# A hybrid backbone block: the RWKV inverse takes its first masked product from LQ by four predicated copies of 32 rows on DVE

## The chip, the cores and the metric

The kernel runs on one core of one Trainium2 chip. The core has five engines that run side by side and wait for each other by semaphores: PE (TensorE: matrix products and transposes), DVE (VectorE), ACT (ScalarE), POOL (GpSimd) and SP (SyncE, which here only issues transfers). Each works through its own list of instructions in order. The metric is the device time of one execution in microseconds (us), the median of several.

## The reference

Two layers over 256 context tokens and 1024 latent tokens of width 1024. Each layer has a modulated RMSNorm, one input projection that feeds three groups, an output projection, and a SwiGLU feed-forward part:

```python
px_a, px_b, px_c = _split(px, (GLA_COLS, SWA_COLS, RWKV_COLS))
oa_c, oa_x = gla_group(...)     # chunked gated linear attention
ob_c, ob_x = swa_group(...)     # windowed softmax attention
oc_c, oc_x = rwkv_group(...)    # RWKV-7, both directions
xx = xx + g1x * (jnp.concatenate([oa_x, ob_x, oc_x], axis=-1) @ w_out[l])
```

The change lies in the RWKV group. Its recurrence, for each of four heads of width 64 and each of two directions, is

```python
sa = jnp.einsum('bhvk,bhk->bhv', S, kkt)
S = S * wt[:, :, None, :] - sa[..., None] * (kkt * at)[:, :, None, :] + vt[..., None] * kt[:, :, None, :]
o = jnp.einsum('bhvk,bhk->bhv', S, rt)
```

## The kernel before

All data is fp32; the big projections are split into a high and a low part (fp32r) and take three products each (`ps_in` for the input projection).

**The RWKV stage** (`rwkv_mixer`, one per layer) works on chunks of 64 tokens, 20 chunks per direction, and takes both directions and all heads together: a tile `[128, 4, 128]` holds four units `u` (two directions by two pairs of heads), with the two heads of a pair in the upper and lower 64 partitions. Inside a chunk the recurrence is a triangular system, and its inverse `X` is built by doubling: blocks of 1, 2, 4, ... rows are joined by masked products.

`prep()` runs once per chunk `i` and works on two chunks at a time, the young one (`i`) and the old one (`i - 1`). For the young one it makes, in this order: the products `AK` by `AK` on PE (`gram`, into `ps_g`), masked by DVE into `LQ`; the first joining step, which needs no product, since for blocks of one row the entries are those of `LQ` itself (the lines that change); and the transpose of `X` in blocks of 32, `XT`. For the old one it makes `MP` (another `gram`). Then come two joining steps for both chunks together, each of four parts that wait for each other: `ps_y` on PE (from `LQ` and `XT`), its copy `y` on ACT, `ps_w` on PE (from `y` and `X`), a predicated copy into `X` on DVE under the mask `lev2`, and again `XT`. Last, for the old chunk alone, the step from 32 to 64 rows (a short `ps_y` and `ps_w`, `KT`, `XF`).

The tiles `X` and `XT` are halves of `X2` and `XT2` `[128, 2, 4, 32]`: partition 32a + s holds row s of diagonal block a, with columns of 32. In `LQ` those diagonal blocks lie at columns `r % 64` of the rows from `r`, a different column offset for rows 0 to 31 and 64 to 95 than for 32 to 63 and 96 to 127. So the four groups of 32 rows have to be taken apart.

`scan()` runs one chunk behind: `ps_r` from `MP` and the values `Vbd` and from `AK` and the state `SBD`; its copy `Rbd` (half on DVE, half on ACT); `ps_r` again from `Rbd` and `XF`; the copies `VU` (DVE) and `Ubd` (ACT); `ps_s` from `VU` and `KT`; and DVE's sum into `SBD`, the state for the next chunk.

**What runs beside it.** The input projection of the other two groups (`in_rest`: `ps_in`, 24 products for each of its column blocks and groups of tokens) fills PE between the steps. Its results are drained by ACT, and some need more work: rotary positions (`t`, `in`, with a product on POOL at L657) and, ten times per layer, a unit of the GLA decay (`in_gla`, L690 to L730: `ps_gl` on PE, `gl_z` on DVE, four functions on ACT with two loads of function tables, `gl_z` and a running sum `gl_u` on DVE).

**What sets the order.** The order on PE in this stage is written by `Weave`: every job is a generator that yields the time it wants to wait, measured by a count `TE.t` of the nominal times of the products placed so far, and the next job taken is the one that is due first. So the number in a `yield` is a guess of how long the other engines need until the next product of this job can start, and PE's list is filled with other jobs' products for as long. `yield 3400` stands between the two `gram` calls and the first `ps_y`. The order on DVE, ACT, POOL and SP is chosen by a scheduler when the program is built; the operations of `prep` and `scan` are given priority (`FIRST`; their calls all show as L177 in the profile).

Of the kernel before, what the change touches and what calls it, by code (L numbers as in the profile page):

```python
# [10 lines left out]
F32 = mybir.dt.float32  # L11
# [27 lines left out]
P = 128  # L39
# [106 lines left out]
def block_kernel(ctx: ExitStack, tc: tile.TileContext, a):  # L146
    nc = tc.nc
    V, S, G, SY = nc.vector, nc.scalar, nc.gpsimd, nc.sync
# [973 lines left out]
    def rwkv_mixer(l, t_first, pool, fpool, pp, spawn):  # L1122
# [7 lines left out]
        lev1 = pool.tile([P, 128], U8, name="lev1")  # L1130
# [19 lines left out]
        f2 = lambda ap: ap.rearrange("p u n -> p (u n)")  # L1150
# [5 lines left out]
        def gram(AK, w_, dst):  # L1156
            V = FIRST[0]
            ps = new([P, 4, P], "ps_g")
            for u in range(4):
                for hs in H:  # L1160
                    TE.matmul(ps[hs, u, :], AK[hs, u, w_, :], AK[hs, u, 0:2, :].rearrange("p s n -> p (s n)"))
            V.tensor_tensor(dst.rearrange("p (d q) n -> p d q n", d=2), ps.rearrange("p (d q) n -> p d q n", d=2),
                            mgr.unsqueeze(2).to_broadcast([P, 2, 2, P]), ALU.mult)
# [3 lines left out]
        def load(i):  # L1167
            b, cc = batch[i], (i, SIGC[i])

            AK = pool.tile([P, 4, 4, 64], F32, name="AK", bufs=4)  # L1170
            for d in range(2):
                SY.dma_start(AK[:, 2 * d:2 * d + 2], d_ab[:, 2 * d:2 * d + 2, cc[d]])
            Dt = pool.tile([P, 4], F32, name="Dt", bufs=4)
            for d in range(2):
                G.tensor_copy(Dt[:, 2 * d:2 * d + 2].unsqueeze(2), Dall[l][:, 2 * d:2 * d + 2, cc[d]:cc[d] + 1])
            b.update(cc=cc, AK=AK, Dt=Dt)
# [6 lines left out]
        def prep():  # L1183

            V, S, G = FIRST
            load(0)
            for i in range(NC + 1):
                yield after(("s", i - 3))
                p = i % 2
                young, old = batch[i] if i < NC else None, batch[i - 1] if i else None  # L1190
                hv = slice(0, 2) if i < NC and i else slice(p, p + 1) if old is None else slice(1 - p, 2 - p)
                if young is not None:
                    if i + 1 < NC:
                        load(i + 1)
                    X, XT = X2[:, p], XT2[:, p]
                    G.tensor_copy(X, eye32.unsqueeze(1).to_broadcast([P, 4, 32]))
                    young["LQ"] = LQ = pool.tile([P, 4, P], F32, name="LQ", bufs=3)
                    gram(young["AK"], 3, LQ)
                    ld = pool.tile([P, 4, 32], F32, name="ld")
                    for r in range(0, 128, 32):  # L1200
                        S.copy(ld[r:r + 32], LQ[r:r + 32, :, r % 64:r % 64 + 32])
                    V.copy_predicated(f2(X), lev1, f2(ld))
                    V.transpose(f2(XT), f2(X))
                if old is not None:
                    cc, Dt, AK = (old[n] for n in ("cc", "Dt", "AK"))
# [12 lines left out]
                                    Dt.unsqueeze(2).to_broadcast([P, 4, P]), ALU.mult)  # L1218
                    old["MP"] = MP = pool.tile([P, 4, P], F32, name="MP", bufs=2)
                    gram(AK, 2, MP)  # L1220
                yield 3400 if young is not None else 0
                both = [(h, b["LQ"]) for h, b in ((p, young), (1 - p, old)) if b is not None]
                for step in range(2):
                    py = new([P, 2, 4, 32], "ps_y")
# [17 lines left out]
                X, XT, LQ, xf = X2[:, 1 - p], XT2[:, 1 - p], old["LQ"], XF[p]  # L1242
# [113 lines left out]
        for rank, gen in ((0, scan()), (1, prep()), (3, finish_all())):  # L1356
            spawn(gen, rank, LEAD[l])
# [582 lines left out]
```

## Time and profile before

| | |
|---|---|
| median of 3 runs | 3725.89 us (3722.07 to 3726.19) |
| profiled execution | 3736.55 us, of which the span of the profile is 3734.3 us |
| PE busy | 3554.6 us, 95% of the span |
| DVE busy | 2378.2 us, 64% |
| ACT busy | 1498.3 us, 40% |
| POOL busy | 706.5 us, 19% |

Busy times are sums over an engine's instructions. Several small products of PE overlap in its array, so many matmuls can share one stretch of busy time. An engine's idle time costs something only where PE, or the work that ends last, waits for it.

### The profile page before, as it was taken

The numbers are of one execution on the slowest core, as the hardware profiler recorded it, in microseconds if no ns is written. First come the engines' busy times: TensorE is split into PE (matmuls) and PEld (weight loads), VectorE is DVE, ScalarE is ACT, GpSimd is POOL, SyncE is SP. The second block draws the span as 40 slices with busy tenths as digits, with TensorE's granted clock in tenths as the row PEclk, the third lists the DMA queues.
The fourth block names the chain that finished last, engine by engine and source line by source line (L and its number), as shares of the span: only waits on it lengthen the run. The fifth ranks groups of instructions, "written<-read, shape, count | busy, mean of one in ns | idle before, by whom it ended". The sixth has DMA issues, their size and how long they took to land. (4 is left out here: it accounts for less than half of the span.)

```text
span 3734.3 us, 76148 instructions
## 1 busy us (share of the span) xinstructions
PE 3554.6 (95%) x30714; PEld 2821.1 (76%) x30714; DVE 2378.2 (64%) x4596; ACT 1498.3 (40%) x3014; POOL 706.5 (19%) x979
## 2 busy tenths in 40 slices
PE   7998999999999999999999998889899999999998
PEld 4767778656688888888888766778777778888787
DVE  4764556556557777746776783455665576666766
ACT  4434543346324333333442553543366153333213
POOL 3122332111323000000332232232211340000002
PEclk9999999999999999999999999999989999999999
DMA  5253443552331333325421234343321332221511
GB/s 183 105 170 101 116 133 95 144 147 84 98 108 58 110 113 112 114 71 197 130 91 58 87 136 151 111 149 93 94 74 53 102 108 94 82 88 57 203 63 62
DMA packets 310767, 405.77 MB, mean 109 GB/s; under 512 B 52880, under 2 KB 210192, under 8 KB 308368
## 3 DMA queue, kind: packets, MB, share of 16 engines
q1 hardware_dynamic: 310416, 400.92, 34.2%
q8 instruction: 242, 3.96, 0.5%
q14 instruction: 109, 0.89, 0.1%
HBM read 290.54 MB, written 105.03 MB: 106 GB/s over the span
## 5 line engine op out<-in xcount | busy, mean ns | idle before, releaser
L160 PE MATMUL ps_in<-h,w_hl 128*128 128x512 f32 (+1 forms) x2928 | 712.1, 384 | 10.4 <-ACT w_hl L412 3.3
L160 PEld LDWEIGHTS ps_in<-h,w_hl 128*128 128x128 f32 x2928 | 490.0, 194 | 128.5 <-issue 43.3
L160 PE MATMUL ps_gu<-f,hl 128*128 128x512 f32 (+1 forms) x2400 | 567.3, 389 | 7.4 <-DVE hl L413 4.1
L160 PE MATMUL ps_d<-g,w_hl 128*128 128x512 f32 (+1 forms) x2688 | 557.5, 369 | 8.4 <-DVE x L1704 5.9
L160 PEld LDWEIGHTS ps_d<-g,w_hl 128*128 128x128 f32 x2688 | 464.2, 189 | 102.2 <-DVE x L1704 10.5
L160 PEld LDWEIGHTS ps_gu<-f,hl 128*128 128x128 f32 x2400 | 442.9, 190 | 101.2 <-DVE hl L413 5.0
L1704 DVE SCALAR_TENSOR_TENSOR x<-ps_d,mods,x 128x512 f32<-128x512 f32 (+1 forms) x448 | 290.7, 683 | 132.3 <-PE ps_d L160 131.8
L160 PE MATMUL ps_gu<-T,hl 128*128 128x512 f32 x1440 | 346.8, 390 | 1.4 <-DVE u L1605 1.4
L160 PEld LDWEIGHTS ps_gu<-T,hl 128*128 128x128 f32 x1440 | 268.7, 188 | 57.6 <-ACT g L412 1.8
L277 POOL TENSOR_TENSOR ada<-ada 128x256 f32<-128x256 f32 x112 | 90.6, 841 | 690.0 <-DMA x<-d_gt 558.3
L365 POOL TENSOR_TENSOR nacc<-nacc,nsq 128x512 f32<-128x512 f32 (+1 forms) x52 | 60.8, 1170 | 758.5 <-ACT nsq L364 743.5
L412 ACT CAST hl<-S 128x512 fp32r<-128x512 f32 x160 | 98.4, 620 | 250.3 <-PE ps_gu L160 156.4
L412 ACT CAST w_hl<-w_raw 128x1024 fp32r<-128x1024 f32 (+1 forms) x100 | 100.9, 1013 | 237.4 <-PE ps_d L160 200.1
L412 ACT CAST hl<-raw 128x512 fp32r<-128x512 f32 x156 | 96.7, 623 | 221.4 <-PE ps_gu L160 194.6
L1044 DVE TENSOR_REDUCE mx<-ps_ss 128x1 f32<-128x640 f32 (+2 forms) x144 | 107.4, 747 | 118.0 <-PE ps_ss L160 117.5
L160 PE MATMUL ps_o<-m,w_hl 128*128 128x512 f32 (+1 forms) x720 | 173.1, 388 | 0.0
L413 DVE TENSOR_TENSOR hl<-S,hl 128x512 fp32r<-128x512 f32 x160 | 109.9, 689 | 65.2 <-ACT hl L412 64.8
L160 PEld LDWEIGHTS ps_o<-m,w_hl 128*128 128x128 f32 x720 | 126.8, 194 | 32.5 <-issue 8.2
L413 DVE TENSOR_TENSOR w_hl<-w_raw,w_hl 128x1024 fp32r<-128x1024 f32 (+1 forms) x100 | 120.1, 1204 | 37.0 <-ACT w_hl L412 36.8
L413 DVE TENSOR_TENSOR pT<-ps_st,pT 128x512 fp32r<-128x512 f32 (+1 forms) x168 | 108.9, 656 | 32.9 <-ACT pT L412 32.4
L160 PEld LDWEIGHTS ps_x<-f,hl 128*128 128x128 f32 x960 | 124.5, 191 | 6.6 <-issue 0.8
L160 PE MATMUL ps_x<-f,hl 128*128 128x256 f32 x960 | 127.1, 283 | 0.0
(354 smaller groups left out, 5993.3 us busy)
## 6 DMA issues: line engine op xcount, KB each, us to landing
w_raw<-in_w_in_dram SPq DMA_DIRECT2D x44, 512.0 KB, 3.8
raw<-in_w_gate_dram SPq DMA_DIRECT2D x44, 512.0 KB, 4.1
raw<-in_w_up_dram SPq DMA_DIRECT2D x44, 512.0 KB, 3.6
x<-d_gt SPq DMA_DIRECT2D x88, 256.0 KB, 3.7
AK<-d_ab SPq DMA_DIRECT2D x80, 256.0 KB, 3.6
w_raw<-in_w_down_dram SPq DMA_DIRECT2D x40, 512.0 KB, 4.2
d_gt<-u SPq DMA_DIRECT2D x68, 256.0 KB, 2.0
d_ab<-W SPq DMA_DIRECT2D x16, 1024.0 KB, 4.1
```

The costliest lines, as they stand in the source:

```text
L160: return nc.tensor.matmul(out, lhsT, rhs, **kw)
L277: G.tensor_tensor(acc[:, s], acc[:, s], ps_[n % 2], ALU.add)
L365: (G if 0 < o < 5 else V).tensor_tensor(self.acc[g0], self.acc[g0], sq[:, :n], ALU.add)
L412: S.copy(dst[:, 0], src)
L413: V.tensor_tensor(dst[:, 1], src, dst[:, 0].bitcast(F32), ALU.subtract)
L1044: V.tensor_reduce(m_, psf[:, :nk * P], AX.X, ALU.max)
L1704: V.scalar_tensor_tensor(x[:, o, g0:g0 + n], ps[:, :n], mods[:, l, s, 40 + o:41 + o], x[:, o, g0:g0 + n], ALU.mult, ALU.add)
```

## The change

The copy of the four diagonal blocks into `ld` on ACT is dropped. Instead of one predicated copy of 128 rows from `ld`, DVE makes four of 32 rows straight from `LQ`, each with its own column offset. The pause that `prep` asks for between the `gram` products and the first `ps_y` goes from 3400 to 2600.

```diff
                     young["LQ"] = LQ = pool.tile([P, 4, P], F32, name="LQ", bufs=3)
                     gram(young["AK"], 3, LQ)
-                    ld = pool.tile([P, 4, 32], F32, name="ld")
                     for r in range(0, 128, 32):
-                        S.copy(ld[r:r + 32], LQ[r:r + 32, :, r % 64:r % 64 + 32])
-                    V.copy_predicated(f2(X), lev1, f2(ld))
+                        V.copy_predicated(X[r:r + 32], lev1[r:r + 32].rearrange("p (u n) -> p u n", n=32),
+                                          LQ[r:r + 32, :, r % 64:r % 64 + 32])
                     V.transpose(f2(XT), f2(X))
...
-                yield 3400 if young is not None else 0
+                yield 2600 if young is not None else 0
```

The new pause moves products on PE in both RWKV stages, and the scheduler's order on the other engines moves with them. Elsewhere the two programs stand in the same order but for a few rows at the beginning of the softmax attention that follows.

On PE, in the iteration for chunk 14 of the first layer, this stood between the products for LQ and MP (`ps_g`) and the scan's last product (`ps_in` is fill; 128x512 is a wide one):

```order
L160 MATMUL ps_g<-AK 64x128 x16
L160 MATMUL ps_in<-h_288,w_hl 128x256 x7
L160 MATMUL ps_r<-Vbd_1818,MP 128x128 x4
L160 MATMUL ps_r<-SBD,AK 128x128 x4
L160 MATMUL ps_in<-h_334,w_hl 128x512 x5
L160 MATMUL ps_y<-XT_1828,LQ 32x32 x32
L160 MATMUL ps_r<-Rbd,XF_1820 128x128 x4
L160 MATMUL ps_in<-h_334,w_hl 128x512
L160 MATMUL ps_w<-X_1827,y 32x32 x32
L160 MATMUL ps_in<-h_334,w_hl 128x512 x4
L160 MATMUL ps_s<-VU,KT 128x128 x4
L160 MATMUL ps_r<-Ubd,LQ 128x128 x4
```

And in the same place of the changed program:

```order
L160 MATMUL ps_in<-h_334,w_hl 128x512 x3
L160 MATMUL ps_r<-Vbd_1818,MP 128x128 x4
L160 MATMUL ps_r<-SBD,AK 128x128 x4
L160 MATMUL ps_in<-h_334,w_hl 128x512 x2
L160 MATMUL ps_y<-XT_1828,LQ 32x32 x32
L160 MATMUL ps_in<-h_334,w_hl 128x512 x3
L160 MATMUL ps_r<-Rbd,XF_1820 128x128 x4
L160 MATMUL ps_w<-X_1827,y 32x32 x32
L160 MATMUL ps_in<-h_334,w_hl 128x512 x2
L160 MATMUL ps_s<-VU,KT 128x128 x4
L160 MATMUL ps_r<-Ubd,LQ 128x128 x4
```

Three wide fill products that stood ahead of the first `ps_y` now stand behind it, ahead of `ps_r<-Rbd`; two of those that stood between `ps_w` and `ps_s` have gone to later places.

On DVE, in the iteration for chunk 3 of the first layer, from LQ to the copy of the second joining step, before (the rows of L703 to L722 belong to a GLA unit, `lev_1792` is the mask `lev1`):

```order
L177 TENSOR_TENSOR LQ<-ps_g,c_mgr 128x512
L177 TENSOR_TENSOR MP<-ps_g,c_mgr 128x512
L177 COPY_PREDICATED X_1827<-lev_1792,ld 128x128
L177 STREAM_TRANSPOSE XT_1828<-X_1827 128x128
L177 COPY Rbd<-ps_r 64x4x64
L703 TENSOR_SCALAR gl_z<-ps_gl,par 128x256
L707 SCALAR_TENSOR_TENSOR gl_z<-gl_z,gl_u 128x256
L712 SCALAR_TENSOR_TENSOR gl_u<-cst,gl_z 128x256
L177 COPY VU<-ps_r 64x512
L718 COPY dD<-gl_e 128x4
L722 TENSOR_TENSOR gl_e<-gl_e,gi 128x256
L177 COPY_PREDICATED X_1827<-lev_1793,ps_w 128x256
```

And in the changed program:

```order
L177 TENSOR_TENSOR LQ<-ps_g,c_mgr 128x512
L177 COPY_PREDICATED X_1827<-lev_1792,LQ 32x128 x4
L177 TENSOR_TENSOR MP<-ps_g,c_mgr 128x512
L177 STREAM_TRANSPOSE XT_1828<-X_1827 128x128
L177 COPY Rbd<-ps_r 64x4x64
L177 COPY VU<-ps_r 64x512
L177 COPY_PREDICATED X_1827<-lev_1793,ps_w 128x256
L177 STREAM_TRANSPOSE XT_1828<-X_1827 128x256
L703 TENSOR_SCALAR gl_z<-ps_gl,par 128x256
L177 TENSOR_TENSOR SBD<-ps_s,tmp 64x4x64 x2
L707 SCALAR_TENSOR_TENSOR gl_z<-gl_z,gl_u 128x256
L712 SCALAR_TENSOR_TENSOR gl_u<-cst,gl_z 128x256
```

MP has moved behind the four copies, and the GLA unit has moved from between `Rbd` and `VU` to either side of `SBD`. Over both layers, other groups' rows stand between `Rbd` and `VU` in 19 of 40 iterations before and in 9 after; L707 stands between the two in six of its twenty places before and in none after, when twelve are behind `SBD` and six between XT and `SBD`.

On PE, the last iteration of the second layer, in which only the old chunk is worked on, before:

```order
L160 MATMUL ps_g<-AK 64x128 x8
L160 MATMUL ps_r<-Vbd_22386,MP 128x128 x4
L160 MATMUL ps_r<-SBD,AK 128x128 x4
L160 MATMUL ps_y<-XT_22396,LQ 32x32 x16
L160 MATMUL ps_r<-Rbd,XF_22388 128x128 x4
L160 MATMUL ps_w<-X_22395,y 32x32 x16
L164 MATMUL ps_f<-cst,fy 128x128 x2
L160 MATMUL ps_s<-VU,KT 128x128 x4
L160 MATMUL ps_r<-Ubd,LQ 128x128 x4
L160 MATMUL ps_y<-XT_22396,LQ 32x32 x16
L160 MATMUL ps_w<-X_22395,y 32x32 x16
```

And in the changed program:

```order
L160 MATMUL ps_r<-SBD,AK 128x128 x4
L160 MATMUL ps_in<-h_20762,w_hl 128x512 x5
L160 MATMUL ps_y<-XT_22356,LQ 32x32 x16
L160 MATMUL ps_r<-Rbd,XF_22348 128x128 x4
L164 MATMUL ps_f<-cst,fy 128x128 x2
L160 MATMUL ps_w<-X_22355,y 32x32 x16
L160 MATMUL ps_in<-h_20762,w_hl 128x512 x4
L160 MATMUL ps_s<-VU,KT 128x128 x4
L160 MATMUL ps_r<-Ubd,LQ 128x128 x4
L160 MATMUL ps_in<-h_20762,w_hl 128x512
L160 MATMUL ps_y<-XT_22356,LQ 32x32 x16
L160 MATMUL ps_in<-h_20762,w_hl 128x512 x5
```

Fifteen wide fill products now stand in this iteration, where there were none; the number of fill products in the whole stage is the same.

## Rows read from the trace of the kernel before

**Rows 1.** Windows, first RWKV stage: us, busy time (instructions) by engine, PE's clock, DMA.

```profile
core 0 of [0], span 3734.3 us
...
255.00:682.00 427.00, 390.32 (x8034) 321.55 (x8035) 234.05 (x637) 181.63 (x438) 118.82 (x196) 0.96 0.38 111
```

**Rows 2.** Waits of PE, first stage: in total, times, longest (us).

```profile
PE ps_y L160 <- DVE XT L177: 11.7, 8, 3.3
PE ps_w L160 <- ACT y L177: 7.3, 7, 1.9
PE ps_s L160 <- DVE VU L177: 6.5, 5, 2.2
...
PE ps_r L160 <- ACT Ubd L177: 3.0, 3, 1.0
```

**Rows 3.** Waits of PE, second stage.

```profile
PE ps_y L160 <- DVE XT L177: 19.4, 9, 3.3
PE ps_r L160 <- ACT Rbd L177: 7.9, 6, 2.1
...
PE ps_w L160 <- ACT y L177: 5.4, 7, 1.3
```

**Rows 4.** Timeline of one iteration: start, us, engine, line, operation, [idle before].

```profile
609.02 0.69 DVE L177 TENSOR_TENSOR LQ<-ps_g,c_mgr 128x512 f32<-128x512 f32 x1 [0.58 <-PE ps_g L160]
...
609.80 1.22 ACT L177 COPY ld<-LQ 32x128 f32<-32x128 f32 x4 [1.33 <-DVE LQ L177]
609.89 0.69 DVE L177 TENSOR_TENSOR MP<-ps_g,c_mgr 128x512 f32<-128x512 f32 x1 [0.18 <-PE ps_g L160]
...
611.12 0.30 DVE L177 COPY_PREDICATED X<-lev,ld 128x128 f32<-128x128 uint8 x1 [0.54 <-ACT ld L177]
...
611.46 0.31 DVE L177 STREAM_TRANSPOSE XT<-X 128x128 f32<-128x128 f32 x1
...
613.60 0.75 PE L160 MATMUL ps_y<-XT,LQ 32*32 32x32 f32 x64
```

**Rows 5.** Tile XF: shortest/median/longest ns, first and last start.

```profile
L177 DVE TENSOR_TENSOR XF<-X,c_eye x80: 235/344/732, 289.0 to 2672.5; 32x128 f32<-32x128 f32 x80
```

**Rows 6.** Timeline, first and last of 13 iterations with little spare time.

```profile
386.82 0.31 DVE L177 STREAM_TRANSPOSE XT<-X 128x128 f32<-128x128 f32 x1
...
388.22 0.75 PE L160 MATMUL ps_y<-XT,LQ 32*32 32x32 f32 x64
...
2630.01 0.31 DVE L177 STREAM_TRANSPOSE XT<-X 128x128 f32<-128x128 f32 x1
...
2631.37 0.75 PE L160 MATMUL ps_y<-XT,LQ 32*32 32x32 f32 x64
```

**Rows 7.** Timeline, a GLA unit ahead of VU.

```profile
370.40 0.43 DVE L707 SCALAR_TENSOR_TENSOR gl_z<-gl_z,gl_u 128x256 f32<-128x256 f32 x1 [2.97 <-ACT gl_u L706]
...
371.59 0.68 DVE L177 COPY VU<-ps_r 64x512 f32<-64x512 f32 x1
...
372.32 1.16 PE L160 MATMUL ps_s<-VU,KT 128*128 128x128 f32 x8 [1.16 <-DVE VU L177]
```

**Rows 8.** Timeline, a load of function tables ahead of the copy y.

```profile
396.72 1.28 ACT L713 ACT_TABLE_LOAD   x1
...
398.88 0.90 PE L160 MATMUL ps_w<-X,y 32*32 32x32 f32 x64 [1.87 <-ACT y L177]
```

**Rows 9.** Timeline of PE at the end of the second stage.

```profile
2660.03 0.33 PE L160 MATMUL ps_y<-XT,LQ 32*32 32x32 f32 x16 [2.30 <-DVE XT L177]
...
2670.76 0.45 PE L160 MATMUL ps_w<-X,y 32*32 32x32 f32 x32 [0.40 <-ACT y L177]
...
2681.82 11.62 PE L160 MATMUL ps_in<-h,w_hl 128*128 128x512 f32 x48
```

**Rows 10.** Timeline, a predicated copy beside the rope product on POOL.

```profile
535.92 1.70 POOL L657 TENSOR_TENSOR in<-in,rope 128x512 f32<-128x512 f32 x1 [2.76 <-DMA t<-in]
...
536.41 1.38 DVE L177 COPY_PREDICATED X<-lev,ld 128x128 f32<-128x128 uint8 x1
```

## The prediction

> **What bounds the kernel now.** I read the page first: TensorE (PE) is busy in almost the whole span, so what counts is the time in which PE stands still. The edited lines run only in the two RWKV stages, one per layer, each about 427 us long; the windows view of the first shows PE busy in 390 us of them, ScalarE (ACT) in 182 us, VectorE (DVE) in 234 us [rows 1]. No engine but PE is near its limit there. What PE does in the stage is fixed: the same products stand in both programs. So the change can only move PE's waits, and the waits view says what they are: in the first layer 11.7 us for the transposed inverse XT, 7.3 us for ACT's copy `y`, 6.5 us for DVE's copy `VU` and 3.0 us for ACT's `Ubd` [rows 2]; in the second 19.4 us for XT, 7.9 us for `Rbd`, 5.4 us for `y` [rows 3]. All of it is some 61 us in 3734, and no single kind is long. The masked copies themselves are seen in one iteration of the timeline [rows 4]: LQ ends at 609.71, four ACT copies make `ld` (1.22 us) while DVE masks MP beside them, the predicated copy takes 0.30 us, the transpose 0.31 us and ends at 611.77, and the product that needs it starts at 613.60. There is 1.83 us to spare, and PE does not wait.
>
> **What the change does to the first step.** ACT loses four copies per iteration, 160 in all, 1.22 us per group. DVE loses one predicated copy of 0.30 us and gains four. The trace has none of 32 rows. The nearest row on the low side is DVE's 32-row subtraction of the same 128 elements at 0.235 us (its shortest), on the high side its median, 0.344 us [rows 5]; between them I take 0.30 us, the present copy's, since the free size is the same and only the rows are fewer. The four then take 1.2 us (0.94 to 1.38). DVE's new order puts MP behind them and ahead of the transpose in most iterations, so its 0.69 us, which lay beside `ld`, now lies in the chain: from LQ's end 0.05 + 1.20 + 0.69 + 0.04 + 0.31, about 2.3 us to the end of XT instead of 2.0 to 2.06 (2.03 to 2.47 by the bounds). The shorter pause also moves the first `ps_y` ahead of three wide fill products. 48 of those take 11.62 us [rows 9], so that is 0.72 us. The spare time shrinks by 1.0 us in each of 40 iterations. I read the spare, from the end of XT to the start of `ps_y`, in all 40: in 27 it is 1.14 us or more, mostly near 1.85, and there nothing happens. In 13 it is less, the first at 387.13 to 388.22, the last at 2630.32 to 2631.37 [rows 6]; the smallest, 0.14 us, is the hand-over itself. Adding up what is missing there (1.02 + 0.14 less the spare) gives 7.3 us of new waits, 4.5 us with the low price of the copy, 9.4 us with the high. In some of the 13 XT was late because `ld` stood behind other ACT work, which can't happen any more: **+6 us**. Queued behind the four copies on DVE are MP, XT and then `Rbd`; `Rbd` isn't wanted until the SBD products end, at about the moment when DVE now comes free, so I add nothing for it.
>
> **What moves with it.** The new pause shifts where the GLA units (`in_gla`, ten per layer, one DVE chain each that has to wait for ACT in its middle) fall into an iteration. Today five of them stand between `Rbd` and `VU` on DVE. The one at 370 us shows the price: DVE holds `gl_z` until ACT has made `gl_u`, `VU` starts only at 371.59, and `ps_s` on PE waits 1.16 us [rows 7]; VU and Ubd together are 9.5 us in the first layer. In the second, some 5 of the 7.9 us for `Rbd` lie ahead of the tail and come the same way. After the change no unit stands between the two. They stand around `SBD` instead, twelve behind it (eleven of them just ahead of the next masked copy), six ahead of it. There they cost too: in the iteration of 398.88 ACT is in a table load of 1.28 us when `ps_y` ends, and `ps_w` waits 1.87 us for `y` [rows 8]. Three of today's five units of that kind in the first layer pay this. So today's price is 9.5 + 5 + 3 x 1.9 + some 2 in the second layer, 22 us; if three in five of the eighteen pay 1.9 us it is 20.5 us: **-2 us**. The ends are far apart: -15 if the waits for VU, Ubd and Rbd go and nothing comes in their place, +12 if all eighteen pay.
>
> **The tail of the second layer.** The fill products run out there: the last iteration has none, and PE waits 2.30, 1.39 and 0.40 us, three times in all from 2660.03 to 2670.76 [rows 9]. The new order still has fill in that iteration, ahead of `ps_y`, `ps_s` and the last `ps_w`. I take the three as covered, **-4 us** (0 to -4.1).
>
> **ACT's relief.** 80 copies per layer at 1.22 us for four are 24 of 182 us, 13% of its work there. Of the 12.7 us that PE waits for `y` I take the same share, **-2 us** (0 to -6; the first `ps_w` also has three more products ahead of it).
>
> **Sum.** +6 - 2 - 4 - 2 = -2 us. The profiled execution took 3736.55 us around a span of 3734.3, so it would take 3734.5; the median of the runs shown is 3725.89, 10.7 us below it, and becomes **3724 us**. 0.2%, about what a measurement of this kernel can tell from no change, is 7.5 us.
>
> **A rule against the row.** In one iteration the predicated copy took 1.38 us instead of 0.30, in exactly the time in which GpSimd ran its rope product [rows 10]; a second of the 40 looks the same. The Trainium skill says why (SBUF — State Buffer, "Who interferes with whom"): VectorE with two SBUF inputs and GpSimd reading SBUF share a read interface, and whoever starts first keeps the other out. By that rule the four copies, which all have two SBUF inputs, offer the lock 1.2 us instead of 0.3 us per iteration. The row agrees; what it would cost here is a rival below.
>
> **The rivals.** *Slower, the GLA units (0.22).* Standing around SBD, each unit's table loads and its wait in DVE's queue meet `y` or the second masked copy, and each of the eighteen costs PE the 1.87 us of the one at 398.88. For it: eleven now stand in exactly that place. Against it: two of the five there today pay nothing. It is +12 + 6 - 4 - 2 = +12, 3738 us; it decides from about 1.6 us per unit on, where the sum passes +7.5. *Faster, the queues come clean (0.28).* With nothing between `Rbd` and `VU` in 31 of 40 iterations (21 now), the waits for VU, Ubd and Rbd go and none replaces them: -15 + 6 - 4 - 2 = -15, 3711 us. For it: they are the best understood waits in the trace. Against it: the units must run somewhere. *The lock (0.07).* If in each of the twenty iterations with a rope product a copy is held 1.08 us longer, that passes the remaining spare of 0.85 us by 0.23 us: 20 x 0.23 = 4.6 us more, 3728 or 3729 us. Against it: only two of 40 copies met one, and GpSimd is idle where they now stand in the iteration shown.
>
> **How the numbers follow.** The forecast, all terms small and of both signs, gets 0.43, with its own range 3716 to 3732. The range takes in most of both rivals, 3708 to 3741. Faster by over 0.2% is the clean-queue case and the forecast's low edge, 0.32; slower the GLA case, 0.22; within 0.2% the rest, 0.46.
>
> **What the new profile would show.** No `ld`; 160 predicated copies near 0.30 us, four in about 1.2 us; XT ending 2.3 us after LQ; waits of `ps_y` for XT at the first step in about a dozen iterations, of 0.2 to 1 us; the VU and Ubd waits of the first layer mostly gone, longer waits of `ps_w` for `y` and of the last `ps_y` for XT; no 2.30 us wait in the tail. ACT's busy time should fall by some 47 us and DVE's rise by about 36 us, neither of which is worth anything by itself. I am wrong if the 32-row copies take far from 0.30 us, if the waits around the GLA units don't keep their total, or if a stage changes in which nothing was edited.

## The result, and the profile after

The changed kernel takes 3746.33 us (3743.11 to 3750.85, four runs) against 3723.98 us for the kernel before on the same chip: a ratio of 1.0057 [1.0044, 1.0070]. It is 22.4 us slower by the medians and some 21 us by the ratio, outside the predicted range, on the side of the rival that was given 0.22.

The page of the profiled execution has the engines' totals.

```profile
span 3749.1 us, 76101 instructions
...
PE 3558.4 (95%) x30714; PEld 2826.6 (75%) x30714; DVE 2425.6 (65%) x4716; ACT 1449.8 (39%) x2854; POOL 703.1 (19%) x979
```

ACT lost 48.5 us of work and DVE gained 47.4; the prediction had 47 and 36. Neither is what the time is made of. The first RWKV stage, in the same window as [rows 1], has PE busy for 6.6 us less of the same 427 us.

```profile
255.00:682.00 427.00, 383.75 (x7951) 318.65 (x7952) 253.85 (x690) 153.89 (x349) 117.11 (x195) 0.95 0.38 110
```

The view of PE's waits (in total, times, longest us) says for what it waited; the first two lines shown are the first stage and answer to [rows 2], the other four the second, as in [rows 3].

```profile
PE ps_y L160 <- DVE XT L177: 23.8, 14, 3.3
PE ps_w L160 <- ACT y L177: 14.8, 6, 3.4
...
PE ps_y L160 <- DVE XT L177: 28.5, 18, 5.0
PE ps_w L160 <- ACT y L177: 10.5, 7, 3.8
...
PE ps_r L160 <- ACT Rbd L177: 2.4, 2, 1.4
PE ps_s L160 <- DVE VU L177: 2.2, 2, 1.5
```

The waits for XT and `y` have grown from 43.8 us in both stages together to 77.6. Those for `VU` and `Ubd` of the first stage are gone, and `Rbd` has fallen from 7.9 to 2.4 us in the second.

The row of the new copies in the view of the tile X (shortest, median, longest ns) shows that their price was not the mistake:

```profile
L177 DVE COPY_PREDICATED X<-lev,LQ x160: 281/297/1273, 260.0 to 2665.3; 32x128 f32<-32x128 uint8 x160
```

The timeline of the iteration at 538 us shows what was (start, us, engine, line, operation, [idle before]); its first row holds both `gram` products:

```profile
534.50 1.96 PE L160 MATMUL ps_g<-AK 64*64 64x128 f32 x32
...
536.11 1.28 POOL L657 TENSOR_TENSOR in<-in,rope 128x512 f32<-128x512 f32 x1 [1.08 <-DMA t<-in]
536.17 1.77 DVE L660 TENSOR_TENSOR t<-t,rope 128x512 f32<-128x512 f32 x1 [3.02 <-DMA t<-in]
...
538.34 0.69 DVE L177 TENSOR_TENSOR LQ<-ps_g,c_mgr 128x512 f32<-128x512 f32 x1
...
538.94 0.68 DVE L661 TENSOR_TENSOR in<-in,t 128x512 f32<-128x512 f32 x1
539.54 0.68 DVE L177 TENSOR_TENSOR MP<-ps_g,c_mgr 128x512 f32<-128x512 f32 x1
...
540.14 1.21 DVE L177 COPY_PREDICATED X<-lev,LQ 32x128 f32<-32x128 uint8 x4
541.38 0.69 DVE L664 TENSOR_TENSOR qk_hl<-in,qk_hl 128x512 fp32r<-128x512 f32 x1
541.99 0.30 DVE L177 STREAM_TRANSPOSE XT<-X 128x128 f32<-128x128 f32 x1
...
542.45 1.03 PE L160 MATMUL ps_y<-XT,LQ 32*32 32x32 f32 x64 [2.83 <-DVE XT L177]
```

A product of the rotary positions (`t`, L660) stands in DVE's list ahead of LQ. It has to wait 3.02 us for the DMA that brings `t`, takes 1.77 us, and LQ, whose `gram` began at 534.50, starts at 538.34 only. Where nothing is ahead, LQ starts 1.14 us after `gram`'s start (in the ninth run below, 525.08 after 523.94). So LQ is 2.7 us late. Two more rows of the same rotary unit (L661, L664) stand between LQ and XT, so that XT ends 3.26 us behind LQ's end and not the usual 2.28, which is 1.0 us more. Late by 3.7 us with some 0.9 us to spare, PE waits 2.83 us. The four copies took 1.21 us, as forecast.

In the kernel before, the same rope product stands behind LQ and MP in this iteration, and LQ starts 1.14 us after `gram` (533.55 after 532.41):

```profile
533.55 0.69 DVE L177 TENSOR_TENSOR LQ<-ps_g,c_mgr 128x512 f32<-128x512 f32 x1 [0.58 <-PE ps_g L160]
...
535.80 0.69 DVE L660 TENSOR_TENSOR t<-t,rope 128x512 f32<-128x512 f32 x1 [0.69 <-DMA t<-in]
...
538.74 0.81 PE L160 MATMUL ps_y<-XT,LQ 32*32 32x32 f32 x64 [0.53 <-DVE XT L177]
```

The wait costs more than itself. The windows view of six microseconds from the middle of the wait on (PE, PEld, DVE, ACT, POOL busy, granted clock, DMA) shows that the granted clock of PE, 1.00 during the wait, falls to 0.50 (1.2 of 2.4 GHz) when PE is at work again:

```profile
541.00:542.00 1.00, 0.00 (x0) 0.00 (x0) 0.95 (x4) 0.00 (x0) 0.00 (x0) 1.00 0.72 264
542.00:543.00 1.00, 0.55 (x45) 0.58 (x49) 0.60 (x3) 0.31 (x1) 0.00 (x0) 0.78 0.20 46
543.00:544.00 1.00, 1.00 (x36) 0.84 (x29) 0.00 (x0) 0.42 (x2) 0.00 (x0) 0.50 0.91 297
544.00:545.00 1.00, 1.00 (x4) 0.80 (x3) 0.00 (x0) 0.00 (x0) 0.00 (x0) 0.50 0.98 175
545.00:546.00 1.00, 1.00 (x7) 1.00 (x6) 0.00 (x0) 0.00 (x0) 0.00 (x0) 0.51 0.89 298
546.00:547.00 1.00, 1.00 (x68) 0.88 (x67) 0.45 (x1) 0.00 (x0) 0.00 (x0) 1.00 0.43 114
```

That is 0.22 + 0.50 + 0.50 + 0.49 = 1.7 us of full-speed work lost behind a wait of 2.8 us.

The same sums over both RWKV stages, from the first `ps_g` to the last `ps_r` of each, one profiled execution per row: PE's idle gaps of over 0.2 us, named by the product that waits, and (1 - granted clock) added up. "t" is how many of the 20 rope products L660 stand in DVE's list just ahead of LQ, at most behind other such rows and the copy XF.

```
                        ratio    t | stages  idle  clock  rest |  y1st   w2nd   y6   VU Rbd Ubd w1st
before                  1       4  |  854.4  70.9  32.3  751.2 |   1.6    8.0  22.9  22.4
after                   1.0057  11 |  875.0  90.0  41.1  743.9 |  26.5   24.8  20.3   5.8
e1  copies, 3400        1.0021   4 |  856.1  75.0  28.6  752.5 |   3.3    7.2  24.4  24.3
e2  ld, 2600            1.0034  11 |  868.3  79.2  44.0  745.1 |  13.0   25.8  19.1   4.7
e3  copies, 3000        1.0074   8 |  872.4  80.6  45.4  746.5 |  10.5   18.7  27.4   9.3
e4  copies, 4200        1.0192   9 |  922.0 112.7  56.5  752.8 |   0.0    8.0  24.2  36.3
e5  after, no loads     0.9952  11 |  839.7  68.0  25.6  746.1 |  31.8    7.6  10.0   4.6
e6  before, no loads    0.9914   4 |  822.1  47.2  24.0  750.9 |   1.8    2.5  23.4   5.8
e7  after, unit 500     1.0047   9 |  860.0  78.5  33.7  747.8 |  16.0    4.7  25.1  13.8
e8  copies twice, 3400  1.0102   4 |  887.8  99.9  36.5  751.4 |  14.1    7.2  23.9  25.9
e9  after, rope 7500    0.9988   3 |  849.0  67.8  37.1  744.1 |   9.4   20.6  22.6   2.9
e10 before, rope 7500   0.9982   5 |  837.0  61.8  20.8  754.4 |   3.2    4.6  13.7  20.1
e11 e9, Ln paired       1.0054   7 |  865.2  79.2  56.2  729.8 |   3.4    8.1  35.1   3.2
e12 e11, 3400           1.0064   3 |  870.8  84.5  50.0  736.3 |   0.0   26.5  10.7  16.8
e13 after, one Ln       1.0093  10 |  877.7  86.5  54.7  736.5 |  12.7    4.3  31.4   5.3
e14 e9, one Ln          1.0004   7 |  850.6  70.3  40.5  739.8 |   4.3    0.0  23.8   3.6
e15 e14, 3400           0.9988   3 |  850.0  62.2  40.8  747.0 |   2.3   13.7  10.1   6.1
```

All in us but the ratio and t; "y1st" is the first `ps_y` on XT, "w2nd" the second `ps_w` on `y`, "y6" the short last `ps_y` on XT, and the last column the waits for `VU`, `Rbd`, `Ubd` and of the first `ps_w` for `y` together. What is left when idle and clock are taken from the stages is 730 to 754 us. The work is nearly the same: the stretches hold 1320 fill products before, 6 fewer after, 18 fewer in runs 11, 13 and 14, 33 more in run 4, at some 0.24 us each; and where the clock is low while PE waits, the loss counts twice (1.3 us before, 2.5 after, 11.6 in run 11). So a stage's length is that work, PE's waits, and the clock that falls behind the waits. Both stages grew by 20.5 us: 19.1 of idle, 8.7 of clock, less 7.3 of the rest. Outside the two stages, where nothing was edited, these executions take between 2867 and 2887 us, so the rows are compared by their stages and not by their whole times.

### The profile page after: what moved, and what is told of

Its sections match the earlier page's. It is cut to its first block, busy times and chain, and to the rows that moved or that the text cites. A ratio compares the mean times of both kernels' runs of the same rounds, so it can differ in the third digit from the quotient of the medians.

```text
span 3749.1 us, 76101 instructions
## 1 busy us (share of the span) xinstructions
PE 3558.4 (95%) x30714; PEld 2826.6 (75%) x30714; DVE 2425.6 (65%) x4716; ACT 1449.8 (39%) x2854; POOL 703.1 (19%) x979
## 5 line engine op out<-in xcount | busy, mean ns | idle before, releaser
L160 PEld LDWEIGHTS ps_o<-m,w_hl 128*128 128x128 f32 x720 | 124.8, 191 | 31.4 <-issue 7.3
L160 PEld LDWEIGHTS ps_y<-XT,LQ 32*32 32x32 f32 x5760 | 63.5, 107 | 91.6 <-issue 78.9
```

What stands on the lines that cost most here:

```text
L160: return nc.tensor.matmul(out, lhsT, rhs, **kw)
```

## The experiments

Each ratio is to the kernel before on the same chip, with its 95% interval.

**The two parts apart, and two other pauses.** Runs 1, 3 and 4 keep the four copies and change the pause (2600 in the changed kernel); run 2 keeps ACT's copies into `ld` with the pause of 2600.

```diff
-                yield 2600 if young is not None else 0
+                yield 3400 if young is not None else 0
```

> The four 32-row copies with the old pause of 3400. Theory P (the shorter pause is the price: it takes 0.7 us of spare time ahead of the first ps_y and puts the GLA and rotary work just ahead of LQ): as before, ratio to before 0.998 to 1.002, first-step waits of ps_y for XT back to 1 to 4 us in all from 26.5, ps_w for y at the second step near 8 us. Rival C (the copies are the price, through 36 us more work on DVE and MP in the chain): ratio 1.004 to 1.006, first-step waits above 15 us.

Measured: 3734.46 us, 1.0021 [1.0004, 1.0039].

> The old ld copies on ACT with the pause of 2600, whose order on PE and DVE is that of the changed kernel apart from the copies. Theory P: slower than before by nearly as much as the change, ratio 1.003 to 1.006, first-step waits 15 to 25 us. Rival C: as before, 0.999 to 1.001, first-step waits under 5 us.

Measured: 3737.65 us, 1.0034 [1.0021, 1.0047].

> The four copies with a pause half way between, 3000. If the loss grows with the spare time taken (theory P, smooth), ratio 1.001 to 1.004 and first-step waits about 8 to 15 us. If it is where the other work falls that counts (rival S), the ratio follows the number of its rows just ahead of LQ on DVE, 13 here, 18 before, 29 in the changed kernel: 0.995 to 1.001.

Measured: 3752.52 us, 1.0074 [1.0058, 1.0091].

> The four copies with a longer pause, 4200. Theory P, smooth: no first-step waits (under 2 us), ratio 0.995 to 1.000. Rival S: 24 rows of other work just ahead of LQ, 21 between LQ and XT, so the waits come back elsewhere and the ratio is 1.000 to 1.005.

Measured: 3798.40 us, 1.0192 [1.0172, 1.0212].

Theory P is near in run 1 (3.3 us of first-step waits, the ratio at its upper edge) and in run 2 (the ratio in its range, 13.0 us of waits below its 15); in runs 3 and 4 both theories miss the ratio. The two parts add up: the pause costs 0.34% with `ld` and 0.36% with the copies, the copies 0.21% at 3400 and 0.23% at 2600. By these medians more than half of the loss is the pause, though the intervals of runs 1 and 2 overlap. It is not the spare time alone that the pause leaves: a pause of 3000 leaves more than 2600 and gains nothing (1.0074 and 1.0057, intervals that overlap), and at 4200 the first `ps_y` never waits, but PE waits 33.7 us for `Rbd` and 20.5 us for the XT of the second step. In the order of DVE's list run 2 has, but for the copies and a dozen rows, that of the changed kernel and run 1 that of the kernel before. So the pause comes with another place for the other jobs' rows; the run with the rope products moved, below, shows what that place is worth.

**The GLA units' function tables left out.**

```diff
-            S.activation(u, u, AF.Ln, bias=1.0)
+            S.activation(u, u, AF.Exp, scale=-1.0)
```

> The changed kernel, with the logarithm of the GLA units (L706) replaced by another exponential, so that no unit loads a function table on ACT; the instruction order on DVE, PE and ACT is otherwise that of the changed kernel, and the GLA decays are other numbers than the reference's. Theory T (the waits of ps_w's second step on ACT's y, 8 us before and 25 us after, come from the table loads of 1.28 us that now stand just ahead of y): these waits fall to 10 us or less, the y0 waits on XT stay near 26 us, and the time falls by some 15 us to a ratio of about 1.001 to 1.002. Rival D (ACT's y is late because DVE's rows of the unit, or PE's, are in front of what feeds it): the waits stay above 20 us and the ratio stays at 1.005 to 1.007.

Measured: 3708.83 us, 0.9952 [0.9935, 0.9969].

> The kernel before with the same replacement (no table loads in the GLA units, other decays). Theory T: the waits of the second ps_w on y fall from 8 us to about 3, those on VU, Ubd and Rbd by some us too; all in all 5 to 10 us less, a ratio of 0.997 to 0.999, so that the step from here to the changed kernel without loads is about +12 us, what the y0 waits alone gained. Rival D: within 2 us of the kernel before, and the step between the two kernels without loads is the +21 us of the two with them.

Measured: 3693.99 us, 0.9914 [0.9895, 0.9934].

Forty loads of 1.28 us were worth 38 us in the one and 33 us in the other kernel, far more than the 15 and 5 to 10 that I expected. The lists of PE and DVE are row for row those of the kernels with loads, so nothing but ACT's work differs. The waits of PE for `y` in the first stage show the direct part, 6.2 us in place of 14.8:

```profile
PE ps_y L160 <- DVE XT L177: 22.2, 14, 3.4
PE ps_w L160 <- ACT y L177: 6.2, 5, 2.0
```

The step between the two kernels is 14.8 us without loads and about 21 with them. So some 6 us of the loss hang on the loads, and the larger part is elsewhere: the y1st waits stay (31.8 against 1.8 us).

**Another place for the GLA units.** The pause behind each direction of a unit, in the changed kernel:

```diff
-            yield 2000
+            yield 500
```

> The changed kernel, its four copies and its pause of 2600 kept, but the pause behind each direction of a GLA unit 500 in place of 2000, so that the unit's rows stand elsewhere in the iterations: 10 foreign rows of DVE just ahead of LQ in all iterations together (29 in the changed kernel, 18 before), and three table loads just ahead of the second y (9 changed, 6 before). Theory S (the loss is where the units' and the other weaved rows land, not the copies or the pause as such): the y0 waits on XT fall from 26 us to 10 or less, the second ps_w's from 25 to 10 or less, and the ratio to before is 0.998 to 1.002. Rival C (the pause of 2600 leaves the chain LQ, X, XT too little spare wherever the units stand): y0 stays above 20 us and the ratio stays above 1.004.

Measured: 3741.30 us, 1.0047 [1.0030, 1.0064]. Neither theory fits: the second `ps_w` now waits 4.7 us, not 24.8, as S says, and yet the ratio is hardly below 1.0057 (the intervals overlap), as C says, and y1st is at 16.0, between the two forecasts. The pause also moved products on PE, so this run doesn't change the units' place alone. The number of foreign rows ahead of LQ, a third of what it was, is not the point: nine rope products still stand there. Of the eleven y1st waits of over 1.2 us in the changed kernel seven have rope rows (L660, L661) among those just ahead of LQ, 18.6 of 26.5 us; three have the closing rows of the RWKV group (L441 to L1336), 4.8 us; one, 1.3 us, has copies that took 2.20 us.

**The copies twice.** At the pause of before, with each copy issued twice (320 of them, in the same places):

```diff
                     for r in range(0, 128, 32):
-                        V.copy_predicated(X[r:r + 32], lev1[r:r + 32].rearrange("p (u n) -> p u n", n=32),
-                                          LQ[r:r + 32, :, r % 64:r % 64 + 32])
+                        for _ in range(2):
+                            V.copy_predicated(X[r:r + 32], lev1[r:r + 32].rearrange("p (u n) -> p u n", n=32),
+                                              LQ[r:r + 32, :, r % 64:r % 64 + 32])
```

> The changed kernel with the pause of before (3400) and each of the four copies issued twice (the second writes the same values again): 1.2 us more of DVE work between LQ and XT in each of 40 iterations, the other rows where they stand in the kernel before. Beside the run with single copies and this pause (ratio 1.0021). If a longer chain costs by its length (theory L: the spare of XT ahead of ps_y is about 1.9 us at this pause and is used up): y0 waits of 10 to 25 us and a ratio of 1.005 to 1.009. If the copies cost by the engine time only where other rows are pressed (theory S): y0 waits below 6 us, ratio 1.002 to 1.004.

Measured: 3763.42 us, 1.0102 [1.0084, 1.0121]. Theory L was right in kind, the ratio even above its range. Its sign of 10 to 25 us was met: y1st is 14.1, and five more first-step waits, 11.8 us, which the profile puts down to ACT, end like most of the others 0.15 us behind XT's end, so that it is 25.9 with them. The first four copies cost 0.21%, four more 0.8%, 30 us for 48 us of DVE time. From LQ's end to XT's end it is then 3.65 us; the kernel before has 2.0 and a spare of 1.85 there, so that next to nothing is left.

**The rope products moved away.** In the changed kernel, and as the mirror in the kernel before, the pause between the rope's DMAs and its product on DVE:

```diff
-                    yield 3500
+                    yield 7500
                     tc.keep_in_program_order(V.tensor_tensor(t1, t1, rp[:, 1, :], ALU.mult))
```

> The changed kernel, but the rope units pause 7500 in place of 3500 between their DMAs and their first product on DVE (L660), so that three rope products in place of eleven stand just ahead of LQ and none has to wait for its DMA there; copies, the pause of 2600, the GLA units and their table loads stand as in the changed kernel. Theory R (ps_y's first step waits because LQ stands in DVE's queue behind a rope product that itself waits for its DMA): the y0 waits on XT fall from 26 us to 10 or less, those of the second ps_w on y stay near 25 us, and the time falls by 12 to 18 us, to a ratio of 1.001 to 1.003. Rival C (at 2600 the chain of 2.3 us behind LQ is too long for the spare left, whatever stands ahead): y0 stays above 20 us, ratio 1.004 to 1.007.

Measured: 3720.71 us, 0.9988 [0.9979, 0.9997].

> The kernel before (ACT's four copies into ld, pause 3400) with the rope units' pause of 7500 in place of 3500: five rope products ahead of LQ (four before), no wait for their DMAs. By theory R there is little to gain, since y0 waits only 1.6 us there: ratio 0.998 to 1.001. If the longer rope pause is a gain of its own, apart from where LQ stands, the ratio is 0.996 or less, and the run on the changed kernel says less for R.

Measured: 3717.73 us, 0.9982 [0.9968, 0.9996].

The view of line L660 has the wait itself. In the kernel before DVE stood idle for the DMA five times there, 12.3 us in all:

```profile
L660 DVE TENSOR_TENSOR t<-t,rope x20: 649/693/1439, 328.7 to 2543.2; 128x512 f32<-128x512 f32 x20
...
  DMA t<-in: 12.3, 5
```

In the changed kernel the lines of this view read

```profile
L660 DVE TENSOR_TENSOR t<-t,rope x20: 673/693/1775, 332.4 to 2572.8; 128x512 f32<-128x512 f32 x20
...
  DMA t<-in: 21.4, 10
```

and in run 9 there is no such idle line. PE's list in the two stages is row for row that of the changed kernel, and DVE's differs by some 20 rows beside the rope's own, so the run moves little else. The timeline of the same iteration in run 9:

```profile
525.08 0.69 DVE L177 TENSOR_TENSOR LQ<-ps_g,c_mgr 128x512 f32<-128x512 f32 x1 [0.58 <-PE ps_g L160]
...
526.03 1.28 POOL L657 TENSOR_TENSOR in<-in,rope 128x512 f32<-128x512 f32 x1 [1.57 <-DMA t<-in]
...
527.25 0.29 POOL L177 COPY X<-c_eye 128x128 f32<-128x128 f32 x1
...
527.58 1.23 DVE L177 COPY_PREDICATED X<-lev,LQ 32x128 f32<-32x128 uint8 x4 [0.93 <-POOL X L177]
...
528.84 0.31 DVE L177 STREAM_TRANSPOSE XT<-X 128x128 f32<-128x128 f32 x1
...
529.30 0.74 PE L160 MATMUL ps_y<-XT,LQ 32*32 32x32 f32 x64 [0.25 <-DVE XT L177]
529.39 0.67 DVE L660 TENSOR_TENSOR t<-t,rope 128x512 f32<-128x512 f32 x1
```

LQ comes at once, the rope product on DVE stands behind XT and waits for nothing, and PE waits 0.25 us in place of 2.83. What is left is POOL, where the rope's other product waits for the same DMA ahead of the unit matrix for X, and so holds the four copies for 0.93 us. In all, y1st fell from 26.5 to 9.4 us, the w2nd waits stayed (20.6), and the time fell by 25.6 us, more than the 12 to 18 forecast. Without that stall the whole change costs nothing that can be told: 0.9988 against 0.9982, with overlapping intervals. The mirror gained 7.7 us, at the low edge of what was expected; so of the changed kernel's 25.6 us some 18 are of its own making. The wait for the DMA seems to cost more than the place alone: in runs 11 and 14 below seven rope products stand just ahead of LQ, DVE waits for a rope DMA not at all in the one and once, 1.1 us, in the other, and y1st is 3.4 and 4.3 us.

**The logarithm paired.** Runs 11 (pause 2600) and 12 (3400), both with the rope pause of 7500, put both directions of a unit through the logarithm together, to halve the loads:

```diff
-        for d in range(2):
...
+        for d, (z, u) in enumerate(zu):
...
             S.activation(u, z, AF.Abs)
             S.activation(u, u, AF.Exp, scale=-1.0)
+        for z, u in zu:
             S.activation(u, u, AF.Ln, bias=1.0)
+        for d, (z, u) in enumerate(zu):
+            e = z
```

> The changed kernel with the rope pause of 7500 and, besides, both directions of a GLA unit put through ACT's logarithm together, so that a unit loads the tables twice, not four times (20 of 40 loads in the two stages gone; the same results). Theory T: against the same kernel without the pairing the second ps_w's waits on y fall from about 25 us to 12 or less and the time falls by 8 to 18 us more; against the kernel before a ratio of 0.996 to 1.000. If a load costs only where it meets y by chance, the remaining 20 may meet it as often: no gain against the unpaired kernel, ratio 1.001 to 1.003.

Measured: 3746.57 us, 1.0054 [1.0039, 1.0069].

> The four copies on DVE, but the pause of before (3400), the rope pause of 7500 and the paired logarithm: the changed kernel's first part without its second, in a weave without the two things that the runs blame. Theory: y0 below 4 us, second ps_w below 8 us, ratio 0.994 to 0.998. If the copies cost their 0.2 per cent and the pairing gives nothing at this pause: 1.001 to 1.003.

Measured: 3747.51 us, 1.0064 [1.0051, 1.0076].

These did not test the loads, as ACT's loads by line in run 11's stages show:

```profile
L706 ACT ACT_TABLE_LOAD x20 | 25.7, 1283 | 0.4
L704 ACT ACT_TABLE_LOAD x10 | 12.8, 1283 | 0.2
L715 ACT ACT_TABLE_LOAD x9 | 11.5, 1283 | 0.2
```

With one more of L716 these are 40, as before: the scheduler put the second direction's exponential behind the first one's logarithm. What run 11 does show, beside run 9, is what the place of the units' rows, on ACT, DVE and PE, is worth: with the same copies, pauses and number of loads, and y1st at 3.4 us, it is 26 us slower; y6 is 35.1 us in place of 22.6, the third `ps_w` waits 10.0 us in place of 0.3, and the clock takes 56.2 us, not 37.1. Three more runs issue the three functions once each over both directions, which leaves nothing to part; the loads of the units are then 20 (run 13: pauses of the changed kernel; 14: rope pause 7500; 15: that and the pause of 3400).

```diff
...
+        S.activation(u2, z2, AF.Abs)
+        S.activation(u2, u2, AF.Exp, scale=-1.0)
+        S.activation(u2, u2, AF.Ln, bias=1.0)
...
```

> The changed kernel with ACT's three first functions of a GLA unit (L704 to L706) issued once over both directions, so that the scheduler can't part them: 20 table loads in the two stages in place of 40, the same results; pauses 2600 and 3500 as in the changed kernel, ten rope products ahead of LQ (eleven there). Theory T (a load costs where it meets y, and half the loads cost about half): the run without loads was 38 us below the changed kernel, so 12 to 20 us less here, ratio to before 1.000 to 1.003, and the second ps_w's waits on y fall from 25 us to 15 or less. Rival P (what costs is ACT's and DVE's longer run of unit work around the loads, which the pairing makes longer): no gain, 1.004 to 1.007.

Measured: 3762.31 us, 1.0093 [1.0072, 1.0115].

> The same with the rope pause of 7500 (seven rope products ahead of LQ, none waiting for its DMA): the changed kernel without the two costs that the runs blame. Both theories have the rope's gain; T: ratio 0.993 to 0.997, 10 us or more below the kernel with the rope pause alone (0.9988). P: 0.998 or more.

Measured: 3727.39 us, 1.0004 [0.9992, 1.0015].

> The four copies with the pause of before (3400), rope pause 7500 and half the table loads; three rope products ahead of LQ. T: 0.992 to 0.996, below both kernels of the case. P: 0.998 or more.

Measured: 3721.60 us, 0.9988 [0.9973, 1.0004].

Theory T, that half the loads cost about half, missed the time in all three: there was no gain, in run 13 a ratio of 1.0093 against the changed kernel's 1.0057. Its direct sign was there (w2nd fell from 24.8 to 4.3 us), but the third `ps_w` waits 12.4 us for `y` instead, y6 31.4 instead of 20.3, and the next `ps_gl` 7.8 us for DVE's `gl_z`; PE's idle time in the stages was 86.5 us, hardly less than 90.0, and the clock took 54.7 us, not 41.1. That is the kind of thing the rival P says, and its bound held in runs 14 and 15, but its range was missed in run 13. The three runs also put the rows of ACT, DVE and PE in another order, so they do not separate the loads from the rows around them; what the longer unit costs by itself was not measured. No version was clearly better than the kernel before with a longer rope pause alone.

## Why the prediction was wrong

**The first step, +6: the term that failed.** Its parts were right. The copy is 0.297 us at the median (0.30 taken), four take some 1.22 in nearly all iterations, XT ends 2.28 us after LQ at the median (2.3), and the spare shrank from 1.85 to 0.94 us. What failed is the sentence that in 27 of 40 iterations there is spare enough "and there nothing happens": in eight of these 27 PE now waits for XT, 17.4 us in all and up to 4.97 us at a time. The 13 that were priced have 7.5 us of new waits, against 7.3 forecast, but partly by luck: three forecast at some 0.8 us each didn't come, and one forecast at 1.0 us came with 2.3. The lateness of XT was taken iteration by iteration from the old trace, with the old order of DVE's list. The part on what moves with the pause followed only the GLA units. It moved the rope products as well, from four to eleven ahead of LQ, and ten of the twenty, not five, now wait for a DMA of their own on DVE. In place of 7.3 us of new waits there were 24.9 (1.6 to 26.5), in 14 places of 0.2 to 5.0 us where a dozen of 0.2 to 1 were expected. Run 2, without the copies, has 11.4 of them; run 1, without the pause, 1.7; so neither half alone, but a late LQ and the shorter spare together. Run 9 moves the rope away and with it go 17.1.

**The GLA units, -2: near in sum.** `VU`, `Rbd`, `Ubd` and the first `ps_w` gave back 16.6 us (22.4 to 5.8) and the second `ps_w` took 16.8 (8.0 to 24.8), in eleven waits of 1.3 to 3.8 us. This is the "GLA" rival's mechanism and it happened, but it paid for itself. The runs without loads, 14.8 us apart in place of some 21, put some 6 us net on it.

**The tail, -4: right in kind, about half the size.** The three waits of 2.30, 1.39 and 0.40 us that were to be covered, the first and last of them in [rows 9], are 1.76, 0 and 0 us now. PE's timeline has the last iteration's fill, as foreseen:

```profile
2680.02 0.33 PE L160 MATMUL ps_y<-XT,LQ 32*32 32x32 f32 x16 [1.76 <-DVE XT L177]
...
2684.42 1.40 PE L160 MATMUL ps_in<-h,w_hl 128*128 128x512 f32 x5
2685.74 0.45 PE L160 MATMUL ps_y<-XT,LQ 32*32 32x32 f32 x32
2686.12 1.16 PE L160 MATMUL ps_r<-Rbd,XF 128*128 128x128 f32 x8
```

The fill covers the wait for `Rbd` but not the first one, which lies ahead of it; 2.3 us.

**ACT's relief, -2.** Run 1 has it without the new pause: all waits for `y` are 10.8 us against 12.3, so 1.5 us.

**A term that was not there: the clock.** Behind waits of one to five microseconds the granted clock often fell to 0.50, as at 542 us, and the two stages lost 8.7 us more by it, beside 19.1 us more of idle. Every term of the sum counted idle time alone.

**The lock rival** did not decide: of the forty groups of four, two took longer than 1.35 us, 1.69 and 2.20, both while POOL worked. The Trainium skill's rule (SBUF — State Buffer, "Who interferes with whom") fits these, and the rope product's 1.77 us against a median of 0.69 fell where POOL ran its own rope product, but moving the rope left such groups (five in run 9) and still took the loss away.

**What stays open:** why the copies cost 0.21% at 3400 (8 us) when the stages of that run are only 1.7 us longer in its profile (that execution, 3726.37 us, was a short one of its run, and the profiled one of the kernel before, 3736.55 us, a long one, so the two profiles can't settle it), why a pause of 3000 gains nothing although fewer rope products stand ahead of LQ and y1st is lower, and what the rows of a longer GLA unit cost.

## What to carry to other kernels

A number that sets the order of one engine moves every job that is woven in, so a spare time read from the old trace belongs to the old order: list what stands ahead of the first link of a tight chain, in the new order, before pricing the links. Look above all for instructions that wait for a transfer of their own, on an in-order engine; here the place where one landed decided more than how long the edited instructions took, and giving it a later place was worth more than the whole change cost. Check in the trace that an experiment did what its code says: a pairing in the code was no pairing on ACT.

## What was not expected of the hardware

A wait of PE of 2.83 us was followed by some 3.4 us at a granted clock of 0.50, 1.7 us of full-speed work; in the kernels of the prediction the clock took 32.3 us beside 70.9 us of idle time and 41.1 beside 90.0, in run 10 20.8 beside 61.8, in run 13 54.7 beside 86.5. Of PE's waits of over 1 us in the stages, 12 of 31 before and 18 of 37 after had a stretch at 0.50 in the 6 us behind them; in 19 of these 30 the loss was 1.7 us, whether the wait was of 1.5 or of 3.5 us. Runs 2 and 7 have nearly the same idle time (79.2 and 78.5 us) and lose 44.0 and 33.7 us by the clock; which waits are followed by a fall was not worked out. Forty table loads of 1.28 us, 51 us of an engine that is 39% busy, were worth 33 to 38 us of the whole.
